# The last unit's store in two halves of two rows each, the first issued while the other rows are still computed

## The chip, the cores and the metric

One core of a Trainium2 chip. The metric is device time in microseconds (us), lower is better. Single executions of either kernel spread over about 2 us, so differences of less than about 1.2 us (0.13%) are not resolved by the times and have to be read from traces.

## The reference

Attention inside windows of 64 positions, with four sequences of 4096 rows of 1536 numbers in float32:

```python
logits = np.einsum('bnwd,bnud->bnwu', q_w, k_w) * scale
attn = np.exp(logits - logits.max(axis=-1, keepdims=True))
attn = attn / attn.sum(axis=-1, keepdims=True)
out = np.einsum('bnwu,bnud->bnwd', attn, v_w)
```

## The kernel before

The 16,384 rows are 32 units of 512 rows. A unit puts four consecutive rows on each of the 128 partitions (`SLOTS` = 4), so a partition's share of the output is 4 x 1536 x 4 = 24,576 bytes, contiguous in memory. GpSimd issues the loads (they convert to 16 bits; SyncE issues the first one of `q`) and the stores of units 0 to 30. VectorE and ScalarE share the scaling of each row slot in three pieces of 512 columns. Only in the last unit do they count their pieces of slots 2 and 3 in `n_e`, three each. SyncE waits for all of them and stores the unit whole:

```python
def told(ins, u, n, j, a):
    if u == N - 1 and n >= 2:
        ins.then_inc(n_e[a], 1)
    else:
        ins.then_inc(f_o[j][n], 1)
# ... (cut)
for u in range(1, N):                      # GpSimd
    hand_over("q", u, q16, m_q, g_q)
    hand_over("k", u, k16, m_k, g_k)
    gp.wait_ge(m_q, u + 1)
    store(u - 1)
    hand_over("v", u, v16, m_v, g_v)
for a in range(2):                         # SyncE
    sy.wait_ge(n_e[a], 3)
sy.dma_start(
    out=rows(of, (N - 1) * UR, SLOTS, SLOTS), in_=slots(outs[(N - 1) % NO], 0, SLOTS, SLOTS)
).then_inc(d_l, 16)
# ... (cut) waits for d_o and d_l, clears the semaphores
```

The softmax here doesn't subtract the row's maximum and nothing guards it: scores larger than these inputs give would overflow.

## Time and profile before

| | before |
|---|---|
| median of its first 3 runs | 943.34 us (943.31 to 943.55) |
| span of the profiled run | 941.3 us |
| DMA engines busy | 90% or more in each of 40 slices but the last (70%) |
| end of the last scaling | 929.21 us |
| issue of the last store | 929.24 us |
| last of the 16 engines done with it | 939.95 us |

The lines are in the prediction below. Two things help in reading them. The store of a unit is cut into one packet per partition and spread over 16 DMA engines, eight packets each. When an engine has written its share, it adds one to the transfer's semaphore; below, that count is called the engine's landing. The transfer is complete when the slowest of the 16 has counted (at 939.945 here; SyncE's wait ends at 939.96). And the queue q0 holds what GpSimd issues, q1 what SyncE issues, but both are served by the same 16 engines.

### The profile page before, as it was taken

What the parts mean: (1) busy time and instruction counts of PE and PEld (TensorE: products, weight loads), DVE (VectorE), ACT (ScalarE), POOL (GpSimd) and SP (SyncE); (2) the same over time, 40 slices, a digit from 0 to 9 for tenths busy, and PEclk for the clock granted to TensorE, in tenths of its full rate; (3) what the DMA queues carried; (4) which work ended last, traced back from release to release, by engine and by line L of the source; (5) the groups of instructions that cost most, each with busy time, mean ns of one, the idle gap of its engine ahead of it and who ended that gap; (6) DMA issues with size and microseconds to landing.
All of it is one profiled execution on the core that took longest, in us unless ns stands there. A gap on an engine that the chain in (4) does not pass through costs nothing. (4 is left out here: it accounts for less than half of the span.)

```text
span 941.3 us, 13141 instructions
## 1 busy us (share of the span) xinstructions
PE 641.9 (68%) x5120; PEld 371.9 (40%) x3584; DVE 288.4 (31%) x517; ACT 336.0 (36%) x642; POOL 334.1 (35%) x225
## 2 busy tenths in 40 slices
PE   0877777666767767768676586676866767757673
PEld 0544444432444433444233442344533444323440
DVE  0233333332323333233322233222333223322232
ACT  0344444333333233333333333333334334233331
POOL 4244433344333342333423334333343333443220
PEclk9999999998889888797888999889789789888997
DMA  9999999999999999999999999999999999999997
GB/s 257 217 216 279 264 237 282 284 279 276 233 275 283 281 281 237 266 282 282 281 245 257 283 281 282 255 246 283 283 280 264 237 284 283 280 277 230 276 320 329
DMA packets 22540, 253.35 MB, mean 269 GB/s; under 512 B 2048, under 2 KB 2048, under 8 KB 10240
## 3 DMA queue, kind: packets, MB, share of 16 engines
q0 software_dynamic: 22240, 246.95, 99.7%
q1 hardware_dynamic: 288, 6.29, 1.7%
q14 instruction: 10, 0.08, 0.0%
q8 instruction: 2, 0.03, 0.0%
HBM read 301.99 MB, written 100.66 MB: 428 GB/s over the span
## 5 line engine op out<-in xcount | busy, mean ns | idle before, releaser
L164 PE MATMUL lt<-xq,xk 128*128 128x256 f16 x1536 | 203.3, 282 | 0.0
L300 POOL COPY v<-vl 128x3072 f32<-128x3072 f32 x31 | 85.2, 2748 | 278.3 <-DMA vl<-in_v_dram 278.3
L192 PEld LDWEIGHTS <-et 128*64 128x64 f16 x512 | 40.5, 131 | 331.6 <-issue 319.4
L152 PE MATMUL tp<-ident,k 128*128 128x128 f32 x768 | 124.9, 297 | 57.9 <-PEq L218 40.5
L164 PEld LDWEIGHTS lt<-xq,xk 128*128 128x128 f16 x1536 | 153.2, 100 | 27.3
L152 PE MATMUL tp<-ident,q 128*128 128x128 f32 x768 | 107.9, 285 | 80.1 <-DVE xq L228 55.8
L112 PE MATMUL sp<-ones,et 128*64 128x1 f16 x512 | 52.6, 178 | 147.8 <-PEq L218 130.6
L152 PEld LDWEIGHTS tp<-ident,q 128*128 128x128 f32 x768 | 85.9, 145 | 120.8 <-issue 120.7
L228 ACT COPY xk<-tp 128x512 f32<-128x512 f32 x96 | 59.6, 620 | 203.2 <-ACTq L218 203.2
L152 PEld LDWEIGHTS tp<-ident,k 128*128 128x128 f32 x768 | 96.0, 152 | 75.1 <-issue 73.1
L300 POOL COPY k<-kl 128x3072 f32<-128x3072 f32 x31 | 85.2, 2748 | 103.1 <-DMA kl<-in_k_dram 103.1
L245 DVE RECIPROCAL rs<-sp 128x1 f32<-128x1 f32 x128 | 21.4, 167 | 323.8 <-DVEq L218 323.2
L300 POOL COPY q<-ql 128x3072 f32<-128x3072 f32 x31 | 85.0, 2743 | 100.0 <-DMA ql<-in_q_dram 99.9
L228 DVE COPY xk<-tp 128x512 f32<-128x512 f32 x96 | 66.5, 693 | 168.2 <-DVEq L218 168.2
L112 PE MATMUL o<-v,et 128*64 128x512 f16 x768 | 117.7, 440 | 0.0
L279 ACT ACTIVATE out<-tp,rs 128x512 f32<-128x512 f32 x64 | 44.0, 687 | 177.4 <-ACTq L218 177.4
L269 ACT ACTIVATE et<-lt,zeros 32x128 f16<-32x128 f32 x256 | 92.0, 359 | 39.4 <-ACTq L218 36.1
L228 ACT COPY xq<-tp 128x512 f32<-128x512 f32 x96 | 56.3, 586 | 126.4 <-ACTq L218 126.4
L112 PE MATMUL tp<-v,et 128*64 128x512 f16 x512 | 100.2, 468 | 0.0
L256 DVE TENSOR_SCALAR out<-o,rs 128x512 f32<-128x512 f32 x128 | 90.4, 747 | 28.6 <-DVEq L218 28.6
L228 DVE COPY xq<-tp 128x512 f32<-128x512 f32 x96 | 66.1, 688 | 83.7 <-DVEq L218 83.7
L112 PE MATMUL lt<-v,et 128*64 128x512 f16 x256 | 64.5, 479 | 0.0
(21 smaller groups left out, 217.6 us busy)
## 6 DMA issues: line engine op xcount, KB each, us to landing
out_dram<-out POOLq DMA_DIRECT2D x31, 3072.0 KB, 61.6
ql<-in_q_dram POOLq DMA_DIRECT2D x31, 1536.0 KB, 54.9
kl<-in_k_dram POOLq DMA_DIRECT2D x31, 1536.0 KB, 54.9
vl<-in_v_dram POOLq DMA_DIRECT2D x31, 1536.0 KB, 54.9
out<-in_q_dram SPq DMA_DIRECT2D x1, 3072.0 KB, 16.7
out_dram<-out SPq DMA_DIRECT2D x1, 3072.0 KB, 10.7
k<-in_k_dram POOLq DMA_DIRECT2D x1, 1536.0 KB, 17.9
v<-in_v_dram POOLq DMA_DIRECT2D x1, 1536.0 KB, 24.3
```

What stands on the lines that cost most here:

```text
L112: return nc.tensor.add_instruction(mybir.InstMatmult(name=nc.get_next_instruction_name(), engine=PE, ins=[low(rhs), low(w)], outs=[low(o)] ...
L152: ins = nc.tensor.transpose(tps[g % 2][:, r, j, :], pairs[:, c * P : (c + 1) * P], ident[:, :])
L164: ins = nc.tensor.matmul(lts[h][:, r, :, :], lhsT=keys(c, h, r, w), rhs=queries(c, h, w), start=(c == 0 and w == 0 and r == 0), stop=(c == ...
L192: ld = nc.tensor.ldweights(w[h], tile_position=(0, P // H * h))
L228: copy(out=dst, in_=tps[g % 2][:, :, :, :]).then_inc(f_c[g % 4], 1)
L245: ve.reciprocal(out=rs[:, n : n + 1], in_=sp[:, n : n + 1]).then_inc(n_d, 1)
L256: ins = ve.tensor_scalar_mul(scaled(u, n, j), bank(n, j), scalar1=rs[:, n : n + 1])
L269: ins = sc.activation(ets[h][s, :, :, t], lts[h][s, :, :, t], EXP, bias=zeros[s, 0:1], scale=scale)
L279: ins = sc.activation(scaled(u, n, j), bank(n, j), COPY, bias=0.0, scale=rs[:, n : n + 1])
L300: gp.tensor_copy(out=dst[:, :, :].bitcast(FP32), in_=landing[x][u % NL][:, :, :].bitcast(FP32)).then_inc(c_l, 1)
```

## The change

The intent is to start the last transfer earlier. Slots 0 and 1 are finished as soon as each of the two engines has finished its first piece of slot 2. So the first half may go at a count of one, and the second at three.

```diff
-        for a in range(2):
-            sy.wait_ge(n_e[a], 3)
-        sy.dma_start(
-            out=rows(of, (N - 1) * UR, SLOTS, SLOTS), in_=slots(outs[(N - 1) % NO], 0, SLOTS, SLOTS)
-        ).then_inc(d_l, 16)
+        last = rows(of, (N - 1) * UR, SLOTS, SLOTS)[:, 0, :]
+        for i, c in enumerate((1, 3)):
+            for a in range(2):
+                sy.wait_ge(n_e[a], c)
+            sy.dma_start(
+                out=last[:, 2 * i * D : 2 * (i + 1) * D],
+                in_=outs[(N - 1) % NO][:, 2 * i : 2 * (i + 1), :].rearrange("p r d -> p (r d)"),
+            ).then_inc(d_l[i], 16)
```

(`d_l` becomes two semaphores, and the final wait is for both.)

More of the change, by code (lines that the diff above doesn't have):

```diff
@@ L76 @@
     d_o = [sem(f"d_o{i}") for i in range(NO)]
-    d_l = sem("d_l")
+    d_l = [sem(f"d_l{i}") for i in range(2)]
     g_q, g_k, g_v = (sem(n) for n in ("g_q", "g_k", "g_v"))
@@ L287, in store, with stored @@
         ).then_inc(d_o[u % NO], 16)
+    def stored(u):
+        return 16 * (u // NO + 1)
     def request(x, u):
@@ L357 @@
         for u in range(NO, N):
-            sy.wait_ge(d_o[u % NO], 16 * (u // NO))
+            sy.wait_ge(d_o[u % NO], stored(u - NO))
             for a in range(2):
@@ L380 @@
             last = max(u for u in range(N - 1) if u % NO == i)
-            sy.wait_ge(d_o[i], 16 * (last // NO + 1))
-        sy.wait_ge(d_l, 16)
+            sy.wait_ge(d_o[i], stored(last))
+        for i in range(2):
+            sy.wait_ge(d_l[i], 16)
         lo, hi = min(s.num for s in sems), max(s.num for s in sems)
```

## The prediction

> **What bounds the kernel now.** I began with the page's busy slices and its DMA queues, since a change to one store can only matter if transfers, or the wait for this one, set the end.
>
> ```profile
> DVE  0233333332323333233322233222333223322232
> DMA  9999999999999999999999999999999999999997
> q0 software_dynamic: 22240, 246.95, 99.7%
> q1 hardware_dynamic: 288, 6.29, 1.7%
> q14 instruction: 10, 0.08, 0.0%
> ```
>
> The 16 DMA engines are full from the second slice on, while VectorE is at two or three tenths; no compute engine is near its limit. Nearly all of that is q0, the transfers that GpSimd issues. The last unit's store is the only one issued by SyncE at the end, on q1. So the kernel is bound by transfers, and the tail is what is left when only stores remain. Next the timeline of the last microseconds (start, duration, engine, line, operation) and SyncE's waits in them:
>
> ```profile
> 926.21 0.75 DVE L256 TENSOR_SCALAR out<-tp,rs 128x512 f32<-128x512 f32 x1 [0.45 <-DVEq L218]
> 926.22 0.69 ACT L279 ACTIVATE out<-tp,rs 128x512 f32<-128x512 f32 x1 [1.04 <-ACTq L218]
> 926.80 0.68 ACT L279 ACTIVATE out<-lt,rs 128x512 f32<-128x512 f32 x1
> 927.80 1.41 DVE L256 TENSOR_SCALAR out<-o,rs 128x512 f32<-128x512 f32 x2 [0.45 <-DVEq L218]
> 929.24 0.35 SPq L373 DMA_DIRECT2D out_dram<-out  x1
> SPq L382 <- DMA out_dram<-out: 10.3, 1, 10.3
> ```
>
> The last VectorE scaling ends at 929.21, SyncE issues the store at 929.24, and then waits 10.3 us for it. Everything after 929.24 is this transfer and the closing of the program. The last multiplication being over, the change aims at exactly this wait. The question is whether the wait is set by when the store is issued or by what the DMA engines still have to do. The table of stretches (columns: stretch, length, busy time of PE, PEld, DVE, ACT and POOL, granted clock, DMA share, GB/s) and the queues in two short windows tell:
>
> ```profile
> 926.00:928.00 2.00, 1.67 (x18) 0.14 (x2) 1.12 (x3) 1.46 (x3) 0.00 (x0) 1.00 0.92 393
> 928.00:930.00 2.00, 0.00 (x0) 0.00 (x0) 1.21 (x2) 0.49 (x1) 0.00 (x0) 1.00 0.29 123
> 930.00:932.00 2.00, 0.00 (x0) 0.00 (x0) 0.00 (x0) 0.00 (x0) 0.00 (x0) 0.85 1.12 455
> 938.50:939.40 0.90, 0.00 (x0) 0.00 (x0) 0.00 (x0) 0.00 (x0) 0.00 (x0) 0.50 0.06 27
> ...
> q0 software_dynamic: 20, 0.25, 28.1%
> ...
> q1 hardware_dynamic: 1, 0.02, 6.3%
> ```
>
> Between 928 and 930 the share falls to 0.29: most engines have finished and wait for the last store, but some still work on q0, the store of the unit before (28.1% of 16 engines in 928.0 to 930.05). And in 938.5 to 939.4 the share is 0.06, one sixteenth: one packet, on one engine, is all that moves. The end is set by a single straggler.
>
> To see which, I followed the trace's records of single DMA packets, chaining each to the engine whose previous packet ended where it starts. Thirteen engines finish the store of the unit before between 927.8 and 929.9 and idle until the last store's first packets at 930.08. Two more finish it at 930.36 to 930.38. One, call it the straggler, finishes at 931.61 and starts the last store at 931.62 with no gap: eight packets of 24,576 bytes (912 ns each), with an instruction fetch between (309 ns, and the packet after it took 1,180 ns). Its last packet ends at 939.47, the increment lands at 939.945, SyncE wakes at 939.96, and the span ends at 941.29. The other engines' increments land from 937.92 on, the second latest at 938.86. The straggler is no accident of the tail: the spread between first and last engine of each store grows from 1.9 us for the first store to 3.9 us for the 31st.
>
> **What the Trainium skill says.** "Perfetto Trace Analysis", section DMA Optimizations, says that splitting DMAs may help "If DMA engines are generally idle". That is the change's hope; the trace agrees for thirteen engines (idle from about 928 to 930.08) and not for the straggler. "DMA: Bandwidth & Descriptors", section Queues, rings and completion order, says each engine goes round-robin, packet by packet, over the queues it has work for, and that a DMA is complete only when all its engines have counted. The trace agrees with the second: 938.86 or 939.945 decides, not 937.92. The same page, section Latency and other measured facts, says two of the 16 engines usually run slower with GpSimd-issued DMAs, perhaps by contention for the descriptor rings. The trace has packets of 967 to 987 ns on q0 in one chain at 924 to 928 where the others take 912, and only 912 on that chain on q1. That fits, and says the lag was collected before this change acts. The section's first-byte latency of about 0.6 us for SyncE's path compares with 0.84 us here, from 929.24 to 930.08.
>
> **The change, part by part.**
>
> The first half waits for one count of each engine, the second for three. The counted operations are those of rows 2 and 3. VectorE's first ends at 926.96 (926.21 + 0.75), ScalarE's first at 926.91. So the first half is issued at about 926.99, which is 2.25 us before the store of now, and its packets start about 0.84 us later, at 927.83. The second half is issued where the whole is now, 929.24, with packets ready at 930.08. The first issue is over by 927.34 (0.35 us), so it does not delay the second. The order of instructions of the two kernels differs on SyncE alone, by one transfer; VectorE, ScalarE, PE and GpSimd do the same in the same order. Nothing before 926.99 should move.
>
> Engines that idle: eight packets of half a row block (12,288 bytes), some 3.7 us from 927.9 on, then eight more to about 935.4 to 936. Their increments come about 2 us earlier. They do not set the end.
>
> The straggler: its work until the end is fixed. It has until 931.61 the rest of q0, and eight partitions' worth of last unit, and it never idles. Getting the first half at 927.83 only lets it mix the two queues; the sum stays. What is added is per packet: 16 packets instead of 8. No half-size store is in this trace. Loads with conversion took 474 ns for 12,288 source bytes and 925 for 24,576, so a half costs 0.512 of a whole. As an estimate, 0.512 x 912 = 467 ns, and 16 x 467 = 7.47 us against 8 x 912 = 7.30: plus 0.18 us. With halves of exactly 456 ns it would be 0, with 474 ns 0.29. One more semaphore packet is 0.01 us, and one more wait on SyncE at the end (28 ns each) 0.03 to 0.06. Sum: 939.945 + 0.18 + 0.01 = 940.13 for the landing, and some 0.05 behind: 0.24 us later in all, between 0.05 and 0.4. On the measured 943.34 us this gives 943.5 us, rounded a little down.
>
> **The rivals.**
>
> *The early half shortens the tail.* If all engines were alike, the idle time of 928 to 930.08 would be filled and the end come about 2 us earlier: 941.4 us. The share of 0.29 in that stretch speaks for it; the straggler's unbroken chain speaks against it, and I see no way round that unless an unprofiled run has no straggler. Then the two engines at 930.37 would be next, and they have no gap either.
>
> *The two queues hinder each other.* Where q1 met q0 on two engines at 930.37, the first packet took 1,726 and 1,455 ns instead of 912. If that happens to the straggler, add 0.5 to 0.8 us: 944.1. Against it: the straggler's own first q1 packet took 912, and at the start of the program q0 and q1 packets alternate on the engines at 925 ns apiece without loss.
>
> *The instruction fetch moves.* It costs the straggler 0.309 + (1.180 - 0.912) = 0.58 us. With other code on SyncE it may fall on another engine or time: 942.9. I give this one in six.
>
> **Range and chances.** The main path gives 943.4 to 943.8. The fetch that leaves and a part of the first rival pull down, to 942.5; queue mixing pulls up, to 944.1. I take 942.4 to 944.2. Every rival's time is within 0.3% of now, so over 2% (18.9 us) in either direction is out of reach: the whole wait for the last store is 10.3 us.
>
> **What would show it.** In the timeline of the changed kernel there should be two SyncE issues, near 927.0 and 929.24. The DMA share in 928 to 930 should rise from 0.29 to about 0.9 or more; the mean of landing times of most engines should fall by some 2 us; yet in the last microsecond one engine should still be moving packets to about 939.6, and SyncE's last wait should end near 940.1. Half-size packets should take 456 to 474 ns. I am wrong if the last landing comes before 939 (the straggler was not fixed by its work, or lost its lag), or after 940.6 (mixing costs more than the packets).

## The result, and the profile after

The changed kernel takes 943.25 us (median of 6 runs, 942.78 to 944.92), the kernel before 943.33 us in 6 runs. The ratio is 1.0, with a 95% interval of 0.9987 to 1.0013. A ratio here is the mean time of one kernel's fast runs over the mean of the other's in the same rounds, so it is not quite the ratio of the medians. The change makes no measurable difference.

The page's busy slices and queues of the changed kernel:

```profile
DVE  0333332332223333133322233322333223332232
DMA  9999999999999999999999999999999999999997
q0 software_dynamic: 22240, 246.95, 99.6%
q1 hardware_dynamic: 432, 6.29, 1.7%
```

There are 144 more packets on q1 for the same 6.29 MB: 128 halves and 16 counts. The timeline and SyncE's wait of the end:

```profile
928.85 0.75 DVE L256 TENSOR_SCALAR out<-tp,rs 128x512 f32<-128x512 f32 x1 [0.45 <-DVEq L218]
929.44 0.68 ACT L279 ACTIVATE out<-lt,rs 128x512 f32<-128x512 f32 x1
929.65 2.56 SPq L379 DMA_DIRECT2D out_dram<-out  x2
930.44 1.41 DVE L256 TENSOR_SCALAR out<-o,rs 128x512 f32<-128x512 f32 x2 [0.45 <-DVEq L218]
SPq L390 <- DMA out_dram<-out: 9.5, 2, 5.9
```

Two issues are merged in the third line; by their records they begin at 929.65 and 931.88. The first is 0.05 us after VectorE's first piece of slot 2 (928.85 + 0.75 = 929.60), the second just behind the last scaling (931.85). The early start is real: 2.2 us.

All of this lies some 2.6 us later than in the profile of before (last scaling at 931.85, there 929.21). That cannot be the change, which does nothing before 929.6; this profiled execution is the slowest of the six, 944.92 us. So the two tails are compared from the end of the last scaling. The stretches that answer to 928 to 930 and 938.5 to 939.4 of before:

```profile
930.60:932.60 2.00, 0.00 (x0) 0.00 (x0) 1.25 (x2) 0.54 (x1) 0.00 (x0) 1.00 1.00 418
938.50:941.30 2.80, 0.00 (x0) 0.00 (x0) 0.00 (x0) 0.00 (x0) 0.00 (x0) 0.50 0.06 26
...
q1 hardware_dynamic: 62, 0.76, 91.1%
q0 software_dynamic: 4, 0.07, 8.6%
```

The hole is filled: a share of 1.00 in place of 0.29, nearly all of it q1. Yet the end looks as before, only longer: from 938.5 to 941.3 the share is 0.06, one engine of 16. By the records of the landings, the median engine finishes 6.5 us after the last scaling instead of 8.6, which is the intended gain. The last one finishes at 941.82, 10.0 us after the last scaling (10.7 before). Its packets follow each other without a gap from 925 to the end; its last packet of the store before begins at 932.53, its first of the last unit at 933.44.

So what this one engine has left to do sets the end. I call it the straggler, and what it is behind, its backlog.

### The profile page after: what moved, and what is told of

Its sections match the earlier page's. It is cut to its first block, busy times and chain, and to the rows that moved or that the text cites. A ratio compares the mean times of both kernels' runs of the same rounds, so it can differ in the third digit from the quotient of the medians.

```text
span 943.1 us, 13144 instructions
## 1 busy us (share of the span) xinstructions
PE 641.1 (68%) x5120; PEld 371.3 (39%) x3584; DVE 288.0 (31%) x517; ACT 335.5 (36%) x642; POOL 334.1 (35%) x225
## 3 DMA queue, kind: packets, MB, share of 16 engines
q1 hardware_dynamic: 432, 6.29, 1.7%
## 5 line engine op out<-in xcount | busy, mean ns | idle before, releaser
L164 PE MATMUL lt<-xq,xk 128*128 128x256 f16 x1536 | 200.5, 280 | 0.0
```

Source lines behind the costliest of these rows:

```text
L164: ins = nc.tensor.matmul(lts[h][:, r, :, :], lhsT=keys(c, h, r, w), rhs=queries(c, h, w), start=(c == 0 and w == 0 and r == 0), stop=(c == ...
```

## The experiments

Theory S says: the straggler comes to the end with a backlog and never idles, so its work sets the end and an earlier start gives it nothing. Two rivals: theory C (cost) says the early start does help the engine that ends last, and splitting costs as much. Theory B (bytes) says all engines together are limited, so that no order of transfers matters. From the traces, with all times in us:

| kernel | last scaling ends | issue of the last store | median engine lands | last engine lands |
|---|---|---|---|---|
| before | 929.21 | 929.24 | 937.84 | 939.95 |
| changed | 931.85 | 929.65, 931.88 | 938.36 | 941.82 |
| split_not_early | 930.35 | 930.38, 930.76 | 939.09 | 940.91 |
| late_two | 930.32 | 931.86 | 940.46 | 941.25 |
| late_five | 930.55 | 935.09 | 943.70 | 944.48 |
| idle_whole | 929.32 | 929.35 | 937.95 | 938.74 |
| idle_halves | 929.43 | 927.24, 929.46 | 935.96 | 936.69 |

### The changed kernel again (after_again)

No edit. What was expected:

> The changed kernel again, on the chip of the three runs beside it. Theory S (straggler): one DMA engine comes to the end with a backlog and never idles, so the end is its remaining work; time within 1 us of before, and in the trace fifteen engines' increments land some 2 us or more before the last one. Theory C (cost): the early half does gain about 2 us for the engine that ends last, and the splitting (second issue, 128 more packets, mixing of two queues) gives it back; then the last engine would show a gap or slow packets worth about 2 us, and all engines would land nearly together. Theory B (bytes): all engines together are limited by memory, so order does not matter; then packets of the last store run slower than 912 ns per 24,576 bytes while many engines are busy.

Measured: 943.43 us, before 943.41 us; ratio 0.9999 (0.9986 to 1.0013). In its trace the last scaling ends at 929.78, the median engine lands at 936.33 and the last at 940.53, 4.2 us apart. S holds and B does not: 15 engines do finish early, and the packets of the last store take 0.46 us each (median), at full rate. In this execution the last landing is 10.75 us after the last scaling, as in the profile of before (10.74): the 0.7 us by which the first profile of the changed kernel was better did not come again, so they show no gain.

### Splitting without the early start (split_not_early)

```diff
-        for i, c in enumerate((1, 3)):
-            for a in range(2):
-                sy.wait_ge(n_e[a], c)
+        for a in range(2):
+            sy.wait_ge(n_e[a], 3)
+        for i in range(2):
```

> The splitting without the early start: two transfers of two rows, both issued after the last row is scaled. Theory S (one engine ends last because it comes with a backlog and never idles, so a transfer's start does not matter within its slack): the straggler pays only for 8 more packets, 0.1 to 0.3 us; the same as before within 1 us. Theory C (the early half gains about 2 us and splitting costs as much): with the gain gone, the cost stands alone, 1.5 to 2.5 us slower than before.

Measured: 943.39 us, before 943.54 us; ratio 0.9997 (0.9983 to 1.0010). Taking the early start away costs nothing, and splitting costs nothing that can be measured. The cost of 1.5 to 2.5 us that C needs is not there. C falls for the real end of this kernel. The trace does show one slow packet, though: the straggler's first half-size packet, right behind its last of q0, took 1.47 us instead of 0.46 (at 931.59). In the two profiles of the changed kernel the straggler's first packet of q1 took 0.46 us. So where the two queues meet, about 1 us can be lost now and then; the times of this run (at most 0.9 us slower, by the interval) leave room for that, but not for C's cost.

### The whole store later (late_two, late_five)

```diff
+        for i in range(7):                      # late_two: 3
+            nc.scalar.activation(
+                idle[:, :], scaled(N - 1, 0, 0), COPY, bias=0.0, scale=1.0
+            ).then_inc(lag, 1)
+            await_(nc.scalar, lag)
+        nc.scalar.sem_inc(n_e[1], 1)
...
-            sy.wait_ge(n_e[a], 3)
+            sy.wait_ge(n_e[a], 3 + a)
```

> The kernel before, with three copies of 512 columns on ScalarE, each waited for, between the last scaling and the issue of the whole last store: the issue should come about 2 us later. S: the straggler is still busy with the store before, so it loses 0 to 0.6 us. C: the issue's time counts in full for all engines, 2 us later.

> The same with seven copies, an issue about 5.5 us later. S: the slack of 1.5 to 4 us (the straggler's backlog when the last store's first packets are there) is used up, the rest shows: 1.5 to 4 us slower than before, and now all engines' increments land within some 2 us of each other as far as they idle. C: 5.5 us slower.

The delays came out smaller than planned, since ScalarE ends its own last piece before VectorE does: the issue is 1.53 us after the last scaling in late_two and 4.54 in late_five. The times are 944.38 us and 947.19 us, against 943.54 us: later by 0.8 us (ratio 1.0009, 0.9996 to 1.0023, so not resolved) and 3.7 us (ratio 1.0035, 1.0021 to 1.0049). The page's list of transfers gives the time from issue to landing. Its line in the profile of before; then late_five's issue and SyncE's wait for it; then the line of idle_whole (the next experiment), which late_two and late_five have in the same words:

```profile
out_dram<-out SPq DMA_DIRECT2D x1, 3072.0 KB, 10.7
```

```profile
935.09 0.35 SPq L380 DMA_DIRECT2D out_dram<-out  x1
SPq L389 <- DMA out_dram<-out: 9.0, 1, 9.0
```

```profile
out_dram<-out SPq DMA_DIRECT2D x1, 3072.0 KB, 9.4
```

By the landing records, late_two and late_five both take 9.39 us from issue to landing, as idle_whole does, where no engine has a backlog. The kernel before takes 10.7. The 1.3 us between is the time for which the last store waited behind the straggler's backlog in that profile. This is the slack: a start that comes up to this much later would not be seen, and an earlier one is not seen at all. S expected 1.5 to 4 us; the measured slack is 1.3 us in the trace and about 0.9 us in the times (4.54 - 3.65), so it is below that, if not by more than the times resolve.

### No backlog (idle_whole, idle_halves)

Both kernels without the store of the last unit but one. The output is wrong. This takes the cause itself away: when the last store is issued, every engine is idle.

```diff
-            store(u - 1)
+            if u < N - 1:
+                store(u - 1)
```

(The final wait for that store goes too.)

> Wrong result on purpose: the kernel before without the store of the last unit but one, so that no engine has a backlog when the last store is issued (its rows of the output stay unwritten). S: the last store now depends on its issue alone. From the profile of before: packets at 930.1, eight of 0.91 us, landing 0.5 us after: 937.9, or 938.5 with an instruction fetch between, so 1.4 to 2 us faster than before. C: the same for this kernel.

> Wrong result on purpose: the changed kernel without the store of the last unit but one. S: with no backlog the early half gives the last engine what the change was meant to give. First half's packets at 927.8, both halves 16 packets of 0.46 us without a gap, landing near 935.8 (936.4 with an instruction fetch): 2.2 us faster than the whole store without the backlog (2.0 to 2.3), and about 3.5 to 4 us faster than before. C and B: no faster than the whole store by more than 0.5 us.

Measured: 942.62 us for the whole store (ratio to before 0.9991, 0.9977 to 1.0004), 940.35 us for the halves (0.9967, 0.9954 to 0.9981). The halves are 2.27 us faster; the single runs do not overlap (941.87 to 942.98 and 939.79 to 940.80). Stretches of both, idle_whole first:

```profile
928.00:930.00 2.00, 0.00 (x0) 0.00 (x0) 1.32 (x2) 0.61 (x1) 0.00 (x0) 1.00 0.00 0
```

```profile
929.00:931.00 2.00, 0.00 (x0) 0.00 (x0) 0.43 (x1) 0.00 (x0) 0.00 (x0) 1.00 1.15 473
```

With nothing else to move, the whole store leaves all DMA engines at 0.00 until its packets come at 930.2; in idle_halves they are full by then. This is the same edit with the same packets, and here it gains the predicted 2.2 us. S is shown: the gain exists, and the backlog of one engine hides it. C and B expected no more than 0.5 us. Leaving the store out also removes the meeting of the two queues, and that could be what hides the gain. The changed kernel's own trace speaks against it: there the straggler finishes q0 before it begins q1, without a gap, and its first packet of q1 takes 0.46 us.

Two sizes were missed. The whole store without the backlog was 0.95 us faster than before instead of 1.4 to 2, and the halves 3.2 us instead of 3.5 to 4. Its last engine lands 0.7 us after the median, since an instruction fetch (309 ns, and longer packets on either side) falls on that engine here too.

### The whole store early (early_whole)

```diff
+        sy.wait_ge(c_l, 3 * (N - 1))
         sy.dma_start(
-            ... in_=slots(outs[(N - 1) % NO], 0, SLOTS, SLOTS)
+            ... in_=slots(outs[(N - 2) % NO], 0, SLOTS, SLOTS)
         ).then_inc(d_l, 16)
```

(The transfer also moves above the waits for `n_e`.)

> Wrong result on purpose: the last store takes the data of the unit before, so that SyncE can issue it whole at about 920, nine microseconds before the last row is scaled; it has nothing to wait for at the end. S: no engine idles any more, but the straggler's work is the same: within 0.7 us of before, the last landing still about 10 us after the end of the last scaling. C: the transfer is unsplit and never waits, so it gains what the change was meant to, 2 us or more. B: no change either.

Measured: 944.86 us, before 943.41 us; ratio 1.0012 (0.9998 to 1.0025). The time is 1.45 us later, so S's "within 0.7 us" was missed. The last landing is at 939.79 (9.3 us after the last scaling), against 939.95 in the profile of before, although the transfer was issued nine microseconds sooner; it is the straggler's last packet of the store *before*. That agrees with S. The time is spoiled by something else:

```profile
SPq L382 <- DMA out_dram<-out: 19.1, 1, 19.1
SPq L382 <- POOLq L377: 1.6, 1, 1.6
```

After the landing, SyncE spends 1.6 us more in its next wait. The closing from last landing to the end of the span takes 3.4 us instead of 1.3. The record shows why: the kernel's closing waits for `gp.drain()` (L377), and GpSimd's DRAIN ends at 941.44, 1.65 us after the last landing of a store that GpSimd issued. In the profile of before the same instruction ends at 933.74, 1.64 us after such a landing (932.10), and long before the last store is done. Here GpSimd's store lands last, so its drain comes on top. As an estimate from these numbers, a closing of 1.3 us would have given about 942.8 us, within what S expected.

### The last store on fifteen engines (fifteen_whole, fifteen_halves)

```diff
+        for i, (lo, hi) in enumerate(((0, 120), (120, P))):
+            sy.dma_start(out=last[lo:hi, :], in_=outs[(N - 1) % NO][lo:hi, :, :] ...
```

> The kernel before, but the last store goes out as partitions 0 to 119 and partitions 120 to 127, so that it should run on 15 engines (8 partitions each) and 8 engines (one more each), without the sixteenth. S, if the straggler is that engine: its 7.3 us of the last store vanish, the end is set by the other engines with 9 packets, 0.5 to 3 us earlier than before; in the trace no engine moves last-store packets alone at the end. S, if the straggler is among the first eight: 0.9 us later. C: 0.9 us later, for one packet more and one issue more. B: no change.

> The changed kernel with each half on fifteen engines in the same way (four transfers). S, if the straggler is the sixteenth engine: now the early half pays, 1 to 4 us faster than before and faster than the whole store on fifteen engines by up to 2 us. C: slower than before by 0.5 to 1.5 us, four issues and more packets. B: no change.

Measured: 952.75 us (ratio 1.0094, 1.0079 to 1.0110) and 945.93 us (1.0028, 1.0014 to 1.0041). No theory expected 9 us. The stretches of the last store, fifteen_whole first, then the kernel before:

```profile
932.00:938.00 6.00, 0.00 (x0) 0.00 (x0) 0.00 (x0) 0.00 (x0) 0.00 (x0) 0.51 0.92 201
```

```profile
932.00:936.00 4.00, 0.00 (x0) 0.00 (x0) 0.00 (x0) 0.00 (x0) 0.00 (x0) 0.50 1.04 444
```

The engines are as busy, but move 201 GB/s instead of 444: a packet of 24,576 bytes takes 1.87 us in the median instead of 0.91, except on one engine that keeps 0.91. The Trainium skill, "SBUF — State Buffer", section Door 1: The DMA port swizzle, says that partitions p and p + 32 share a port. Runs of eight consecutive partitions would then set two engines on the same ports (0 to 7 and 32 to 39, for instance) at half the rate each, and 88 to 95 alone would find their ports free. This fits the doubled packets and the one fast engine, but it is argued, not tested. The attempt to relieve the straggler changed something larger, so these two runs decide nothing about S.

### Where the backlog comes from (sync_stores_whole)

```diff
     def store(u):
-        nc.gpsimd.dma_start(
+        nc.sync.dma_start(
```

(The store moves from GpSimd's loop to SyncE's, behind the same wait.)

> The kernel before, with all stores of whole units issued by SyncE and not by GpSimd (the loads stay with GpSimd). It asks where the backlog is collected. S with the lag coming from GpSimd-issued stores: the straggler's packets of stores take 912 ns, the spread of the stores' landings no longer grows after the middle of the run, 0 to 3 us faster. S with the lag coming from the loads or from something else on that engine: spread and time as before. Mixing two queues all through the run may change when loads arrive, so up to 5 us either way would not surprise.

Measured: 953.62 us, before 943.54 us; ratio 1.0104 (1.0089 to 1.0120). The page's transfers and, from the stretches, what becomes of the end:

```profile
out_dram<-out SPq DMA_DIRECT2D x32, 3072.0 KB, 18.5
vl<-in_v_dram POOLq DMA_DIRECT2D x31, 1536.0 KB, 55.0
...
930.00:943.00 13.00, 9.79 (x95) 3.99 (x45) 4.23 (x10) 7.18 (x15) 2.75 (x1) 1.00 0.05 21
```

Stores on a queue of their own land in 18.5 us instead of 61.6. They overtake the loads: the last `v` is there at 930.8 (917.1 before), the last scaling ends at 943.95, and from 930 to 943 the DMA engines stand nearly still (a share of 0.05). That is the 10 us (12.7 us in the profiled execution, the slowest of the four).

For the backlog the records say something useful. I take the distance between the last and the last but one engine to land, for the loads of `q` and `k`. In the kernel before it grows from about 0.06 us (load landing at 746 us) to about 0.8 (891 us). With the stores on SyncE it has reached 1.36 us by 270 us already and stays at 1.4 us over the same time, 1.39 to 1.42. For the loads of `v`, however, it is 4 to 5 us. The stores' own landings, which S's expectation was about, spread over 1.5 to 3.5 us from the third on, without growing late in the run, and the last store lands on all 16 engines within 0.14 us, 8.7 us after the last scaling. So in this one execution there was no growth late in the run once GpSimd did not issue the stores, but a lag of one engine remains, seen in the loads, which GpSimd still issues. What makes it slow is left open.

## Why the prediction was right

The time, 943.5 us against a measured 943.25 us, and the verdict were right, and so was the reason; the 0.2 us between are below what the runs resolve. For the same cause the forecast that the change costs 0.24 us is neither shown nor refuted. The time alone would not have told the main path from the second and third rivals, whose 944.1 and 942.9 us lie in the stated range too; the traces and the pair without a backlog do.

- *The bound.* That a single straggler sets the end was shown by idle_whole and idle_halves: without the backlog the same edit gains 2.27 us.
- *The early start.* 2.25 us predicted, 2.22 measured.
- *Half-size packets.* 467 ns was the estimate; the median is 464. Sixteen make 7.42 us, against 7.30 for eight whole ones, 0.12 instead of 0.18 us more.
- *Idle engines.* About 2 us earlier was right: 2.1 us for the median engine, and a DMA share of 1.00 in the hole.
- *First rival, a shorter tail.* It was rejected because of the straggler's unbroken chain. Had there been no straggler, its 2 us would have been right.
- *Second rival, the two queues hinder each other.* In both profiles of the changed kernel the straggler's chain shows no packet above 1 us where the queues meet. In split_not_early it does: one packet took 1.47 us instead of 0.46. So the 0.5 to 0.8 us of this rival can happen to the straggler; it did not in the changed kernel's traces, and the times would not show it.
- *Third rival, the fetch moves.* It stayed: 313 ns at 934.82 in the changed kernel, and the fetch falls in the tail in idle_whole and idle_halves too.

Two points of the prediction were poor. It expected the last landing near 940.1 and called anything after 940.6 a refutation; the profiled execution landed at 941.82. The mark was set in absolute time, as if the backlog were the same in every execution. It is not: the store of the last unit but one is spread over 3.9 us in the profile of before and 6.2 us in that of the changed kernel, and measured from the last scaling the last landing came sooner (10.0 us against 10.7), not later. Already at the last load of `v`, before the change acts, the last engine landed 0.95 us after the next one in the profile of before, 2.04 us in that of the changed kernel and 1.61 us in after_again, whose last landing, 940.53, is just within the mark. And the statement that a straggler's time is fixed "until 931.61" took one trace's number for a property of the kernel; the late runs put the slack at about 1 us.

Four readings in it are loose, and none carries the argument. The DMA share is full from the first slice on, not the second. Of the thirteen engines that were to idle from about 928, three still worked on q0 until 929 to 929.9. The landings of the last store begin at 937.75; 937.92 is the thirteenth of the 16. And what it says of a DMA's completion stands on that page under "Why a DMA increments its semaphore by 16 and not by 1", not in the section that it names.

## What to carry to other kernels

Before starting a transfer earlier, look at which of the 16 DMA engines ends last and whether it ever idles: a low mean share before the transfer only tells that *most* engines wait. If the last one has a backlog, an earlier start fills the others' holes and moves nothing; it pays where that engine too would have been idle. A quick test is to delay the transfer, or to remove the work in front of it, and see whether the end follows.

## What the Trainium skill lacked or had wrong

- "Perfetto Trace Analysis", DMA Optimizations, advises to split where DMA engines are generally idle. The share fell to 0.29 here, and splitting gained nothing, because one engine had a backlog; with a share of 0.00 it gained 2.27 us. This section does not say that the last engine decides.
- "DMA: Bandwidth & Descriptors", Latency and other measured facts, says that two of the engines are usually slower with GpSimd's transfers, without a size. Here the spread of a store's landings grew from 1.9 us to 3.9 us over the run, and to 6.2 us in another execution. With the stores on SyncE one engine still came 1.4 us (`q`, `k`) and 4 to 5 us (`v`) after the next, so stores by GpSimd are not the whole of it; the loads were still GpSimd's.
- The same page, Queues, rings and completion order, has each engine go round-robin over its queues. In early_whole the straggler's packets of q0 and q1 do alternate. In the changed kernel the straggler began three more packets of q0 (930.70, 931.62 and 932.53) after other engines had begun q1 at 930.5, and its first of q1 at 933.44. The page lets one of its packets hold several descriptors; whether a packet of the trace is one of these, and so whether this goes against the page, the runs do not tell.
- No page gives a time for an instruction fetch in the middle of a transfer: 0.31 us for the fetch itself, and with the longer packets beside it the engine landed 0.7 us after the median one in idle_whole.
- "SBUF — State Buffer" gives the ports but does not warn that a transfer over 15 engines can set two of them on one port. The packets took 1.87 us in the median instead of 0.91, and the kernel 9 us longer. That this is the ports' doing is an inference.
- No page says how long GpSimd's drain lasts behind its own transfers: it ended 1.64 us after their last landing in the profile of before and 1.65 us in early_whole, where the time showed it.
